# Softmax times values by groups of four query tiles, and a fixed order of VectorE and ScalarE in the last two products

## The chip, the cores and the metric

The kernel runs on one core of a Trainium2 chip. Its engines work side by side and wait for each other by semaphores: TensorE (PE; its weight loads are listed apart as PEld), VectorE (DVE), ScalarE (ACT), GpSimd (POOL) and SyncE (SP), which here issues nearly all DMA transfers. The metric is the device time of one execution in microseconds, from a median of several executions. Less is better.

## What is computed

One layer of a hybrid encoder over 1024 positions of width 1024, in float32. What the change touches is the chunked attention (8 heads of 64, chunks of 64 positions, each query sees its own chunk and 8 before) and the last norm:

```python
def chunked_rel_attention(q, k, v, rel_bias):
    ...
    scores = jnp.einsum('bnqhd,bnkhd->bnhqk', qc, kb).astype(jnp.float32) * (dh ** -0.5)
    scores = scores + bias[None, None]
    scores = jnp.where(valid[None, :, None, None, :], scores, jnp.float32(-1e30))
    p = jax.nn.softmax(scores, axis=-1).astype(v.dtype)
    out = jnp.einsum('bnhqk,bnkhd->bnqhd', p, vb)
    ...
        mixed = rms_norm(mixed.reshape(b, s, N_GROUPS, GROUP_DIM), g).reshape(b, s, MIX_WIDTH)
        x = x + jnp.einsum('bse,ed->bsd', mixed, w_out[l])
        hdn = jnp.einsum('bsd,df->bsf', rms_norm(x, mlp_norm_g[l]), w_up[l])
        hdn = jnp.square(jax.nn.relu(hdn))
        x = x + jnp.einsum('bsf,fd->bsd', hdn, w_down[l])
    return rms_norm(x, final_norm_g)
```

## The kernel before, in words

Precision is kept by splitting a float32 operand into a high and a low part (`split`, L51 to L53: ScalarE copies the high part, VectorE subtracts) and multiplying in two or three passes (`mm3`, L63 to L66). The 1024 positions are 8 tiles of 128.

**The attention stage** lies between 140 and 395 us. Eight heads are four pairs `p` with `j` = 0, 1; a step `i` is one query tile `t` of one head, 64 steps in all. For a step, `scores(i)` makes the products of queries and keys in PSUM, `softmax(i)` adds the bias, takes the row's maximum (VectorE, tile `st`) and the exponentials (ScalarE, L485, tile `pr`). `turn(i)` transposes `pr` in blocks of 128 x 128 on TensorE (L506, tile `pt`), and copies them as a high part `pth` (ScalarE, L510) and a low part `ptl` (VectorE, L511). A query tile sees at most five key tiles, so there are one to five blocks per step. `values(m)` multiplies them with the values: `v` holds a value tile's high and low part side by side as weights, and the moving operand is `pth` and then `ptl`. Before, it takes two query tiles at a time: `pth` and `ptl` have two buffers of 1280 columns, ordered by the distance of key and query tile, and for each key tile there are two products, of 256 columns (384 for the first of a block). The upper and lower halves of the result `av` are added (`ol` on ScalarE, L539; `ya` on VectorE, L540). For a block of two query tiles there are 4, 8, 12 or 12 products, depending on how many key tiles lie before it.

The tiles `pt`, `av` and two tiles of the group norm (`ms`, `R`; L417, L431) share the PSUM tag "PT", which has two buffers that are handed out in turn. The next tile but one waits until the readers of the first are done.

Between the steps stands a filler: projections of the next pairs and of the convolution (tiles `k`, `q`, `cg`, `xh`, `bg`, products of 512 columns), of which `fill_to` calls so many that they last through the 64 steps. Their weights are loaded by `Proj.load` and split into `wh` and `wl`. For the pairs' keys and queries the raw weights go into the buffers that `kc` and `qc` of the pair before last leave free (`expand`, L398 to L403). A scheduler then orders each engine's queue by its own estimate of durations, so the order of the code is not the order on the engine; within a queue an engine works strictly in order. A stretch of code can be exempted (`manual_schedule`): there the named engines keep the code's order.

**The last stage** (from about 800 us) multiplies the hidden layer with `w_down` in blocks; `PLAN` lists seven products per block of hidden columns, each for four tiles of 128 rows, twelve products of 512 columns per row tile in the last block. In the last two products of the last block, the sum of a row tile is complete after `add` (L876). `finish` (L1172 to L1185) then takes the squares (ScalarE, L1166), the scaled sum (VectorE, L1176), the power -1/2 (GpSimd, L1178, tile `rf`), writes the two halves of the output tile `o` (VectorE, L1184) and sends them.

Of the kernel before, what the change touches and what calls it, by code (L numbers as in the profile page):

```python
# [8 lines left out]
F32 = mybir.dt.float32  # L9
# [21 lines left out]
def trunk(ctx, tc, x, mix_g, w_in, rb_rev, conv_w, sg_ln_g, sg_ln_b, sg_w, sg_b,  # L31
# [104 lines left out]
    def acc_tile(name, tag=None):  # L136
        if tag is None:
            ring["i"] += 1
            tag = ring["tags"][ring["i"] % len(ring["tags"])]
        return psA.tile([P, 1024 if tag == "S" else HALF], F32, tag=tag, bufs=2,  # L140
                        name=name)[:, :HALF]
# [346 lines left out]

    def turn(i):
        p, j, t, kb0, nfar = where(i)  # L490
        if t % 2 == 0:
            pts[i // 2] = [AP_.tile([P, 1280], F32R, tag=a, bufs=2, name=f"{a}{i}") for a in ("pth", "ptl")]
            for d in ((1, 3), (3,), (), ())[t // 2]:
                for a in pts[i // 2]:
                    G.memset(a.bitcast(F32)[:, d * 256:d * 256 + P], 0.0)
        pth, ptl = pts[i // 2]
        tq = t % 2
        nb = t - kb0 + 1
        pr = prs.pop(i)
        for d0, d1 in ((0, min(nb, 4)), (4, nb)):  # L500
            if d1 <= d0:
                continue
            pt = psA.tile([P, HALF], F32, tag="PT", bufs=2, name=f"pt{i}{d0}")
            for d in range(d0, d1):
                b = nb - 1 - d
                PE.transpose(pt[:, (d - d0) * P:(d - d0 + 1) * P], pr[:, b * P:(b + 1) * P], ident)  # L506
            src = pt[:, 0:(d1 - d0) * P].rearrange("p (d m) -> p d m", m=P)
            dh = pth.rearrange("p (d m) -> p d m", m=256)[:, d0:d1, tq * P:(tq + 1) * P]
            dl = ptl.rearrange("p (d m) -> p d m", m=256)[:, d0:d1, tq * P:(tq + 1) * P]
            A.activation(dh, src, AF.Copy)  # L510
            V.tensor_tensor(dl, src, dh.bitcast(F32), op=ALU.subtract)  # L511

    def values(m):
        p, j, tb = m // 8, m // 4 % 2, m % 4 * 2
        pth, ptl = pts.pop(m)
        av = acc_tile(f"av{m}", "PT")
        kbs = [tb] + [kb for kb in range(max(0, tb - 4), tb)] + [tb + 1]
        for i, kb in enumerate(kbs):
            d0 = max(0, tb - kb)
            q0 = max(0, kb - tb)  # L520
            lhs = v2[p, kb // 4][:, kb % 4, j, :]


            for ph, pt in ((0, pth), (1, ptl)):
                first = i == 0 and ph == 0
                if d0 == 4:
                    rhs = pt[:, 1024:1280].rearrange("p (i c) -> p i c", c=P)
                    dst = av.rearrange("p (i c) -> p i c", c=256)[:, :, 0:P]
                elif q0:
                    rhs, dst = pt[:, P:3 * P], av[:, P:3 * P]  # L530
                else:
                    cnt = 3 if first else 2
                    base = 0 if first else min(d0 * 256, 512)
                    rhs = pt[:, base:base + cnt * 384].rearrange("p (i c) -> p i c", c=384)
                    rhs = rhs[:, :, d0 * 256 - base:d0 * 256 - base + P]
                    dst = av[:, 0:cnt * P].rearrange("p (i c) -> p i c", c=P)
                PE.matmul(dst, lhsT=lhs, rhs=rhs, start=first, stop=(i == len(kbs) - 1 and ph == 1))  # L537
        ol = tmp(f"ol{m}", m=256)[0:HD]
        A.activation(ol, av[HD:P, 0:256], AF.Copy)  # L539
        V.tensor_tensor(ya[p][j * HD:(j + 1) * HD, tb * P:(tb + 2) * P], av[0:HD, 0:256], ol, op=ALU.add)  # L540
        if j == 1 and tb % 4 == 2:
            hf = tb // 4
            gnq.append((hf, group_norm(ya[p][:, half(hf)], p, f"a{p}{hf}", lsum[p, hf])))

    def split_mixed(c, hf, y):
# [37 lines left out]
    def sgu(u, between):  # L583
        sgw = raw_tile([P, 4, P], "sgw")
        load(sgw, sg_w.rearrange("g t s -> t g s"))
        ps = acc_tile("sgwT")
        for g in range(4):
            PE.transpose(ps[:, g * P:(g + 1) * P], sgw[:, g, :], ident)
        wsT = tmp("wsT").rearrange("p (g t) -> p g t", g=4)
        A.activation(wsT, ps.rearrange("p (g t) -> p g t", g=4), AF.Copy)  # L590
        G.affine_select(out=wsT, in_=wsT, pattern=[[0, 4], [1, P]], compare_op=ALU.is_ge,
                        fill=0.0, base=0, channel_multiplier=-1)
        wsh, wsl = [AP_.tile([P, 4, P], F32R, tag="P", bufs=3, name=f"wsT{a}") for a in "hl"]
        split(wsT, wsh, wsl)
        lnr = raw_tile([P, 2, 256], "lnr")
        load(lnr[:, 0, :], sg_ln_g.partition_broadcast(P))
        load(lnr[:, 1, :], sg_ln_b.partition_broadcast(P))
        ln = AP_.tile([P, 2, 256], F32, tag="P", bufs=3, name="ln")
        V.tensor_copy(ln, lnr)

        ws = load_moving(C_SU + 256, 256, "ws", lambda j, kk, m: [
            AP_.tile([P, 5, 256], F32R, tag=t_, bufs=2, name=f"ws{t_}{j}")[:, 0:kk] for t_ in ("pth", "ptl")])
        vh = [big("VY", [P, 2, NT, HD], F32R, f"vh{i}") for i in range(2)]
        vl = [big("VY", [P, 2, NT, HD], F32R, f"vl{i}") for i in range(2)]
        for t in range(NT):
            ps = token_proj(t, ws, 256, f"sv{t}")
            gv = tmp(f"gv{t}", m=256)
            A.activation(gv, ps, AF.Gelu)
            bs = sm.tile([P, 6], F32, tag="bs", name="bs")
            V.bn_stats(bs, gv)  # L610
            mv = sm.tile([P, 2], F32, tag="mv", name="mv")
            V.bn_aggr(mv, bs)
            r = rstd_of(mv[:, 1:2], 1, 1.0)
            V.tensor_scalar(gv, gv, mv[:, 0:1], r, op0=ALU.subtract, op1=ALU.mult)
            V.tensor_tensor(gv, gv, ln[:, 0], op=ALU.mult)
            V.tensor_tensor(gv, gv, ln[:, 1], op=ALU.add)
            g4 = gv.rearrange("p (i g e) -> p i g e", i=2, g=2)
            for i in range(2):
                split(g4[:, i], vh[i][:, :, t, :], vl[i][:, :, t, :])
        ws = load_moving(C_SU, 256, "wu", place_w("wu"))  # L620
        u += [big("VY", [P, 4, 256], F32, f"u{i}") for i in range(2)]
        for t in range(NT):
            ps = token_proj(t, ws, 256, f"su{t}")
            A.activation(u[t // 4][:, t % 4, :], ps, AF.Gelu)
        tc.keep_in_program_order(A.preload_act_table_set("exp_and_others"))
        between()
        for g in range(4):
            ps = acc_tile(f"sg{g}")
            i, j = g // 2, g % 2
            mm3(ps, wsh[:, g, :], wsl[:, g, :], vh[i][:, j].rearrange("p a b -> p (a b)"),  # L630
                vl[i][:, j].rearrange("p a b -> p (a b)"), True, True)
            for hf in range(2):
                us = u[hf][:, :, g * HD:(g + 1) * HD]
                pv = ps[:, hf * 256:(hf + 1) * 256].rearrange("p (a b) -> p a b", b=HD)
                V.scalar_tensor_tensor(us, pv, cols[:, 14 + g:15 + g], us, op0=ALU.add, op1=ALU.mult)
# [87 lines left out]
    for i in range(64):  # L723
# [3 lines left out]
        turn(i)  # L727
        a, b = target(i), target(i + 1)
        fill_to((a + b) / 2)
        if i % 2 == 0 and i >= 2:  # L730
            values(i // 2 - 1)
        if i + 2 < 64:
            scores(i + 2)
        fill_to(b)
# [9 lines left out]
            next(norm)  # L744
        if p == 3 and k in (5, 6):
            split_half(0, (k - 5,))
    values(31)
    fill_to(1000)
    gn_all((0,))
    sgu_rows(u, 0)  # L750
# [417 lines left out]
    def early_half(t, k):  # L1168
        square(t, k)
        V.tensor_scalar(sums[t][:, 2:3], sums[t][:, k:k + 1], 1.0 / D, EPS, op0=ALU.mult, op1=ALU.add)  # L1170

    def finish(t, k):  # L1172

        ss = sums.get(t)
        square(t, k)
        V.scalar_tensor_tensor(ss[:, 3:4], ss[:, k:k + 1], 1.0 / D, ss[:, 2:3], op0=ALU.mult, op1=ALU.add)  # L1176
        r = sm.tile([P, 1], F32, tag="rf", name="rf")
        G.tensor_tensor(r, ss[:, 3:4], mhalf[:, 0:1], op=ALU.pow)  # L1178
        o = E_.tile([P, D], F32, tag="o", bufs=2, name=f"o{t}")
        for i in (k, 1 - k):  # L1180
            if t + 1 == NT and i != k:
# [15 lines left out]
        ready[n] = [down_ops(PLAN[s][0], p) for p in BLOCKS[b]]  # L1197

    load_down(BLOCKS[0], (1,))
    banks = {}  # L1200
    for n, (b, s) in enumerate(steps):
        if n + 1 < len(steps):
            prep(n + 1)
# [7 lines left out]
        m, which, start, (i, k) = PLAN[s]  # L1211
        ops = ready.pop(n)
        last = b == len(BLOCKS) - 1
        for u in range(4):
            sl = slice(u * P, (u + 1) * P)
            if start:
# [2 lines left out]
            for j, (ho, wo_) in enumerate(ops):  # L1219
                mm3(ps, ho[:, 0, sl], ho[:, 1, sl], wo_[:, 0], wo_[:, 1], start and j == 0, j == len(ops) - 1,  # L1220
                    skip_group_check=True)
            t = 4 * i + u
            add(acc[t][:, half(k)], ps, acc[t][:, half(k)])
            if last and m in (2, 7):
                early_half(t, k)
            if last and m == 7 and t + 1 == NT:
                V.tensor_tensor(acc[t][:, half(k)], acc[t][:, half(k)], gfin[:, half(k)], op=ALU.mult)
            if last and m in (3, 4):
                finish(t, k)


_INS = ["x", "mix_norm_g", "w_in", "rel_bias", "conv_w", "sg_ln_g", "sg_ln_b", "sg_w", "sg_b",
# [24 lines left out]
```

## Time and profile before

| | |
|---|---|
| median of 3 runs | 1120.9 us (1120.43 to 1121.08) |
| profiled execution | 1118.65 us, span 1116.9 us |
| busy: PE, DVE, ACT, POOL | 98%, 67%, 49%, 7% |
| PE, mean granted clock | 0.992 |
| PE idle behind a named wait, largest | 4.2 us at the start, 3.7 us in two waits of transposes |
| PE's last product starts | 1105.72 us |

The profile is one execution, taken by the hardware. A row of the timeline has the start and the duration in us, the engine, the line, the operation, output <- inputs, and the form; in brackets stands how long the engine was idle before, and what it then waited for. Durations of matmuls are modelled and overlap the next one, so the distance between starts says what a product costs. The span ends some 4 us behind the last vector instruction, with the last output written.

### The profile page before, as it was taken

The numbers are of one execution on the slowest core, as the hardware profiler recorded it, in microseconds if no ns is written. First come the engines' busy times: TensorE is split into PE (matmuls) and PEld (weight loads), VectorE is DVE, ScalarE is ACT, GpSimd is POOL, SyncE is SP. The second block draws the span as 40 slices with busy tenths as digits, with TensorE's granted clock in tenths as the row PEclk, the third lists the DMA queues.
The fourth block names the chain that finished last, engine by engine and source line by source line (L and its number), as shares of the span: only waits on it lengthen the run. The fifth ranks groups of instructions, "written<-read, shape, count | busy, mean of one in ns | idle before, by whom it ended". The sixth has DMA issues, their size and how long they took to land.

```text
span 1116.9 us, 14983 instructions
## 1 busy us (share of the span) xinstructions
PE 1090.4 (98%) x5377; PEld 911.8 (82%) x5377; DVE 746.9 (67%) x1430; ACT 551.5 (49%) x1094; POOL 73.2 (7%) x131
## 2 busy tenths in 40 slices
PE   7999999999999999999999999999999999999996
PEld 6889987887888788887888888888878888888884
DVE  5526477667676761569766656564499978869775
ACT  5434376555664630467555555555544433434442
POOL 1101023101021210000000000000000000000001
PEclk8999999999999999999999999999999999999998
DMA  7523013021120143452543535353698545263303
GB/s 244 184 68 80 1 24 88 18 53 47 43 58 23 39 151 131 151 208 104 177 172 122 189 115 196 113 189 125 250 340 280 196 165 188 86 207 103 96 20 150
DMA packets 83197, 145.16 MB, mean 130 GB/s; under 512 B 6050, under 2 KB 41652, under 8 KB 83124
## 3 DMA queue, kind: packets, MB, share of 16 engines
q1 hardware_dynamic: 82548, 142.38, 37.8%
q10 hardware_dynamic: 576, 1.84, 0.4%
q8 instruction: 42, 0.69, 0.3%
q14 instruction: 31, 0.25, 0.1%
HBM read 98.58 MB, written 41.42 MB: 125 GB/s over the span
## 4 chain that ended last, share of the span: by engine, by line
PE 85%; DVE 7%; DMA 4%; ACT 2%; issue 1%; POOL 0%; SPq 0%; POOLq 0%; DVEq 0%; ACTq 0%
PE uA L66 5%; PE uA L65 5%; PE uA L64 5%; PE dA L66 5%; PE dA L64 5%; PE dA L65 4%; PE dB L64 3%; PE dB L66 3%; PE dB L65 3%; PE av L537 3%; PE uC L64 2%; PE uC L66 2%; PE uC L65 2%; PE o L64 2%; PE o L65 2%; PE o L66 2%
## 5 line engine op out<-in xcount | busy, mean ns | idle before, releaser
L52 ACT ACTIVATE ho<-hr 128x512 fp32r<-128x512 f32 x112 | 69.0, 623 | 140.7 <-PE dA L66 51.2
L64 PE MATMUL dA<-wo,ho 128*128 128x512 f32 x256 | 99.7, 390 | 0.8 <-ACT ho L52 0.8
L66 PE MATMUL dA<-wo,ho 128*128 128x512 f32 x256 | 99.3, 390 | 0.5 <-DVE ho L53 0.5
L65 PE MATMUL dA<-wo,ho 128*128 128x512 f32 x256 | 99.5, 389 | 0.0
L53 DVE TENSOR_TENSOR ho<-hr,ho 128x512 fp32r<-128x512 f32 x112 | 76.8, 690 | 15.7 <-ACT ho L52 15.7
L64 PE MATMUL dB<-wo,ho 128*128 128x512 f32 x192 | 74.8, 390 | 0.0
L66 PE MATMUL dB<-wo,ho 128*128 128x512 f32 x192 | 74.8, 390 | 0.0
L65 PE MATMUL dB<-wo,ho 128*128 128x512 f32 x192 | 74.7, 389 | 0.0
L53 DVE TENSOR_TENSOR wo<-wd,wo 128x512 fp32r<-128x512 f32 x96 | 65.6, 689 | 2.3 <-ACT wo L52 2.3
L52 ACT ACTIVATE wo<-wd 128x512 fp32r<-128x512 f32 x96 | 58.8, 619 | 10.1 <-DVE wd L879 6.2
L485 ACT ACTIVATE pr<-s,st 128x640 f32<-128x640 f32 (+2 forms) x64 | 42.3, 661 | 36.9 <-DVE st L480 26.6
L64 PEld LDWEIGHTS dA<-wo,ho 128*128 128x128 f32 x256 | 48.0, 188 | 11.3 <-ACT ho L52 1.5
L66 PEld LDWEIGHTS dA<-wo,ho 128*128 128x128 f32 x256 | 48.0, 188 | 11.1 <-DVE ho L53 1.1
L65 PEld LDWEIGHTS dA<-wo,ho 128*128 128x128 f32 x256 | 48.1, 188 | 9.9
L510 ACT ACTIVATE pth<-pt 128x512 fp32r<-128x512 f32 (+2 forms) x96 | 40.0, 435 | 32.1 <-PE pt L506 31.4
L876 DVE TENSOR_TENSOR acc<-dA,acc 128x512 f32<-128x512 f32 x64 | 43.8, 690 | 16.7 <-PE dA L66 15.0
L511 DVE TENSOR_TENSOR ptl<-pt,pth 128x512 fp32r<-128x512 f32 (+2 forms) x96 | 45.2, 487 | 12.9 <-ACT pth L510 11.9
L64 PE MATMUL o<-woh,mxh 128*128 128x512 f32 x128 | 50.6, 399 | 0.0
L66 PE MATMUL o<-woh,mxl 128*128 128x512 f32 x128 | 50.0, 391 | 0.0
L65 PE MATMUL o<-wol,mxh 128*128 128x512 f32 x128 | 50.0, 390 | 0.0
L1178 POOL TENSOR_TENSOR rf<-ssf,mhalf 128x1 f32<-128x1 f32 x8 | 4.4, 551 | 617.4 <-DVE ssf L1176 617.4
L876 DVE TENSOR_TENSOR hid<-uC,v 128x512 f32<-128x512 f32 x15 | 10.4, 691 | 51.5 <-PE uC L66 51.5
(344 smaller groups left out, 3083.0 us busy)
## 6 DMA issues: line engine op xcount, KB each, us to landing
wr_u<-in_w_up SPq DMA_DIRECT2D x32, 512.0 KB, 4.3
wd<-in_w_down SPq DMA_DIRECT2D x32, 512.0 KB, 4.6
wr_o<-in_w_out SPq DMA_DIRECT2D x8, 512.0 KB, 4.3
xr<-in_x SPq DMA_DIRECT2D x8, 512.0 KB, 4.9
hs<-h SPq DMA_DIRECT2D x8, 512.0 KB, 3.7
acc<-hs SPq DMA_DIRECT2D x16, 256.0 KB, 6.5
out_y<-o SPq DMA_DIRECT2D x16, 256.0 KB, 2.1
x<-in_x SPq DMA_DIRECT2D x7, 512.0 KB, 3.9
```

Source lines behind the costliest of these rows:

```text
L52: A.activation(hi, raw, AF.Copy)
L53: V.tensor_tensor(lo, raw, hi.bitcast(F32), op=ALU.subtract)
L64: PE.matmul(ps, lhsT=sh, rhs=mh, start=start, stop=False, **kw)
L65: PE.matmul(ps, lhsT=sh, rhs=ml, start=False, stop=False, **kw)
L66: PE.matmul(ps, lhsT=sl, rhs=mh, start=False, stop=stop, **kw)
L485: A.activation(pr[:, :b - a], s[:, a:b], AF.Exp, bias=st[:, 2:3], accum_out=lsum[p, t // 4][:, lc:lc + 1])
L510: A.activation(dh, src, AF.Copy)
L511: V.tensor_tensor(dl, src, dh.bitcast(F32), op=ALU.subtract)
L537: PE.matmul(dst, lhsT=lhs, rhs=rhs, start=first, stop=(i == len(kbs) - 1 and ph == 1))
L876: V.tensor_tensor(out, a, b, op=ALU.add)
L1178: G.tensor_tensor(r, ss[:, 3:4], mhalf[:, 0:1], op=ALU.pow)
```

## The change

`values` takes four query tiles at a time. `pth` and `ptl` become two tags each, one for the first half of a head's query tiles (13 blocks of 128 columns) and one for the second (22), one buffer each. In the second half, the block of distance `d` of query tile `q` stands at column block 1 + 4d + q, with a block of zeros at 0 and at 21, so that the products for the first and the last key tile also have at least 256 columns. In the first half the blocks are ordered by key tile, with one block of zeros (at 11). For each key tile there are again two products, now of 256, 384 or 512 columns; the moving operand reads its blocks at steps of 1, 4 or 5 blocks, and the result is one run of columns. There are 16 blocks of products in place of 32. `ol` and `ya` work on 512 columns. `values(m)` is called every fourth step.

In the last two products VectorE and ScalarE keep the order of the code. `finish` is taken apart: `rate` (scaled sum and power) of a row tile comes ahead of the `add` of the next one, `finish` (the two writes) behind it.

```diff
+        hf, tq = t // 4, t % 4
+        if tq == 0:
+            pts[i // 4] = [AP_.tile([P, (22 if hf else 13) * P], F32R, tag=f"{a}{hf}", bufs=1, name=f"{a}{i}")
+                           for a in ("pth", "ptl")]
+            for a in pts[i // 4]:
+                for z in (0, 21) if hf else (11,):
+                    G.memset(a.bitcast(F32)[:, z * P:(z + 1) * P], 0.0)
...
-                b = nb - 1 - d
+                b = nb - 1 - d if hf else d
...
+            dh, dl = [blocks(a, *((1 + 4 * d0 + tq, 4) if hf else (tq, 3)), d1 - d0) for a in (pth, ptl)]
...
+    def blocks(a, first, step, count):
+        n = a.shape[1] // P
+        a = a.rearrange("p (n m) -> p n m", m=P)
+        return a[:, first:min(n, first + step * (count - 1) + 1):step]
...
-        kbs = [tb] + [kb for kb in range(max(0, tb - 4), tb)] + [tb + 1]
+        kbs = [tb] + [kb for kb in range(max(0, tb - 4), tb + 4) if kb != tb]
         for i, kb in enumerate(kbs):
             lhs = v2[p, kb // 4][:, kb % 4, j, :]
+            q0, q1 = max(tb, kb), min(tb + 4, kb + 5)
             for ph, pt in ((0, pth), (1, ptl)):
+                if kb == tb + 3:
+                    rhs, dst = blocks(pt, *((0, 4) if hf else (11, 1)), 2), av[:, 2 * P:4 * P]
+                elif kb == tb - 4:
+                    rhs, dst = blocks(pt, 17, 4, 2), av[:, 0:2 * P]
                 else:
+                    rhs = blocks(pt, *((1 + 4 * (q0 - kb) + q0 - tb, 5) if hf else (3 * kb + q0, 1)), q1 - q0)
+                    dst = av[:, (q0 - tb) * P:(q1 - tb) * P]
...
-            AP_.tile([P, 5, 256], F32R, tag=t_, bufs=2, name=f"ws{t_}{j}")[:, 0:kk] for t_ in ("pth", "ptl")])
+            AP_.tile([P, 4, 256], F32R, tag=f"{t_}{j}", bufs=1, name=f"ws{t_}{j}")[:, 0:kk] for t_ in ("pth", "ptl")])
...
-        if i % 2 == 0 and i >= 2:
-            values(i // 2 - 1)
+        if i % 4 == 0 and i >= 4:
+            values(i // 4 - 1)
...
+        if n + 2 == len(steps):
+            man.enter_context(tc.manual_schedule(engines={mybir.EngineType.Activation, mybir.EngineType.DVE}))
...
+            if whole:
+                rate(*whole[0])
             add(acc[t][:, half(k)], ps, acc[t][:, half(k)])
...
             if last and m in (3, 4):
-                finish(t, k)
+                square(t, k)
+                whole.append((t, k))
+                if len(whole) > 1:
+                    finish(*whole.pop(0))
+    rate(*whole[0])
+    finish(*whole.pop())
+    man.close()
```

What this does to the engines' queues at two places follows. The first is ScalarE where the heads of pair 1 begin, before the change. `pr` are exponentials (of the next pair's first query tiles from `pr_2040` on), `pth` copies of transposed blocks (the last query tile of pair 0 is copied from `pt_2042` and `pt_2049`), `wh_k` the split of the key weights of pair 2, loaded into `kc`:

```order
L510 ACTIVATE pth_1990<-pt_2042 128x4x128
L52 ACTIVATE wh_k_1967<-kc_1717 128x1024
L510 ACTIVATE pth_1990<-pt_2049 128x128
L485 ACTIVATE pr_2083,lsum_2029<-s_2059,st_2080 128x256
L510 ACTIVATE pth_2085<-pt_2091 128x128
```

The same place with the change:

```order
L512 ACTIVATE pth_1834<-pt_1990 128x4x128
L512 ACTIVATE pth_1834<-pt_1997 128x128
L485 ACTIVATE pr_1988,lsum_1977<-s_1978,st_1985 128x128
L52 ACTIVATE wh_k_1933<-kc_1689 128x1024
L485 ACTIVATE pr_2031,lsum_1977<-s_2007,st_2028 128x256
L512 ACTIVATE pth_2033<-pt_2037 128x128
```

The second copy of the last query tile moved from behind the weights' split to ahead of it. The other place is VectorE in the last two products, for two row tiles in the middle, before the change (`acc` sums, `ssf` the scaled sum of squares, `o` the output):

```order
L876 TENSOR_TENSOR acc_7553<-dB_9798,acc_7553 128x512
L1176 SCALAR_TENSOR_TENSOR ssf_9624<-ssf_9624 128x1
L1184 SCALAR_TENSOR_TENSOR o_10018<-acc_7553,rf,gfin 128x512 x2
L876 TENSOR_TENSOR acc_7555<-dB_9812,acc_7555 128x512
L1176 SCALAR_TENSOR_TENSOR ssf_9642<-ssf_9642 128x1
L1184 SCALAR_TENSOR_TENSOR o_10041<-acc_7555,rf,gfin 128x512 x2
```

And with it:

```order
L878 TENSOR_TENSOR acc_7361<-dB_9606,acc_7361 128x512
L1188 SCALAR_TENSOR_TENSOR o_9820<-acc_7359,rf,gfin 128x512 x2
L1177 SCALAR_TENSOR_TENSOR ssf_9432<-ssf_9432 128x1
L878 TENSOR_TENSOR acc_7363<-dB_9620,acc_7363 128x512
L1188 SCALAR_TENSOR_TENSOR o_9843<-acc_7361,rf,gfin 128x512 x2
```

The writes of a row tile moved behind the add of the next one.

## Rows read from the trace of the kernel before

**Rows 1.** The page, busy us, share of the span, instructions of an engine:

```profile
PE 1090.4 (98%) x5377; PEld 911.8 (82%) x5377; DVE 746.9 (67%) x1430; ACT 551.5 (49%) x1094; POOL 73.2 (7%) x131
```

**Rows 2.** Who waited for whom, TensorE, whole span: total us, times, longest:

```profile
PE xT L218 <- DVE xn L231: 4.2, 1, 4.2
PE pt L506 <- DVE ptl L511: 3.7, 2, 1.9
PE uA L66 <- DVE a1l L53: 1.4, 1, 1.4
```

**Rows 3.** The view of tile av: duration ns (min/median/max), first and last start, forms:

```profile
L537 PE MATMUL av<-pth,v x144: 278/283/522, 145.9 to 392.6; 128*128 128x256 f32 x112, 128*128 128x384 f32 x32
...
L537 PE MATMUL av<-ptl,v x144: 274/283/415, 146.2 to 392.7; 128*128 128x256 f32 x144
L539 ACT ACTIVATE ol<-av x32: 382/382/385, 146.8 to 393.1; 64x256 f32<-64x256 f32 x32
L540 DVE TENSOR_TENSOR ya<-av,ol x32: 406/417/419, 147.2 to 393.9; 64x256 f32<-64x256 f32 x32
```

**Rows 4.** Timeline of TensorE at a block of four products and the scores behind it:

```profile
145.93 0.42 PE L537 MATMUL av<-pth,v 128*128 128x384 f32 x1
146.19 0.27 PE L537 MATMUL av<-ptl,v 128*128 128x256 f32 x1
...
146.54 0.34 PE L463 MATMUL s<-kh,q 128*128 128x384 f32 x1
146.71 0.34 PE L464 MATMUL s<-kl,q 128*128 128x384 f32 x1
```

**Rows 5.** Timeline of TensorE, last products of two row tiles:

```profile
1081.24 0.39 PE L66 MATMUL dA<-wo,ho 128*128 128x512 f32 x1
...
1105.72 0.39 PE L66 MATMUL dA<-wo,ho 128*128 128x512 f32 x1
```

**Rows 6.** Timeline of VectorE in the tail:

```profile
1081.66 0.69 DVE L876 TENSOR_TENSOR acc<-dA,acc 128x512 f32<-128x512 f32 x1 [1.02 <-PE dA L66]
...
1105.68 0.16 DVE L1176 SCALAR_TENSOR_TENSOR ssf<-ssf 128x1 f32<-128x1 f32 x1 [0.85 <-ACT sq L1166]
1106.50 1.42 DVE L1184 SCALAR_TENSOR_TENSOR o<-acc,rf,gfin 128x512 f32<-128x512 f32 x2 [0.67 <-POOL rf L1178]
...
1109.44 0.69 DVE L876 TENSOR_TENSOR acc<-dA,acc 128x512 f32<-128x512 f32 x1
```

**Rows 7.** The chain of waits, 186 to 200 us (start, us, what):

```profile
186.29 5.91 DMA kc<-in_w_in
...
192.22 1.07 ACT wh_k L52
...
193.32 1.22 DVE wl_k L53
194.54 0.21 DVE ptl L511
...
194.80 0.33 PE pt L506
```

**Rows 8.** Timelines of VectorE, ScalarE and TensorE at both heads' changes:

```profile
194.66 0.74 DVE L432 SCALAR_TENSOR_TENSOR ya<-Ra,cols,ya 128x512 f32<-128x512 f32 x1
...
198.40 0.64 ACT L409 ACTIVATE sqa<-ya 128x512 f32<-128x512 f32 x1
...
199.87 0.95 PE L417 MATMUL msa<-onesel,sqa 128*128 128x2 f32 x8
...
258.37 0.33 PE L506 MATMUL pt<-ident,pr 128*128 128x128 f32 x1 [1.80 <-DVE ptl L511]
...
262.65 1.05 PE L417 MATMUL msa<-onesel,sqa 128*128 128x2 f32 x8
```

**Rows 9.** The chain of waits at the end of the attention stage:

```profile
382.40 0.88 DVE ptl L511 x2
...
390.80 2.17 PE av L537 x12
```

**Rows 10.** Stretches there: us, busy us of engines, granted PE clock, DMA:

```profile
384.80:388.80 4.00, 2.01 (x18) 1.61 (x16) 3.92 (x8) 3.89 (x8) 0.00 (x0) 1.00 0.37 131
388.80:392.20 3.40, 3.40 (x14) 3.11 (x15) 2.31 (x4) 1.81 (x3) 2.55 (x1) 0.50 0.10 26
```

More of the change, by code (lines that the diff above doesn't have):

```diff
@@ L490, in turn @@
         p, j, t, kb0, nfar = where(i)
[L491 to L497, printed above, removed]
+        hf, tq = t // 4, t % 4
[5 more added lines that the diff above has]
+                    G.memset(a.bitcast(F32)[:, z * P:(z + 1) * P], 0.0)
+        pth, ptl = pts[i // 4]
         nb = t - kb0 + 1
@@ L504, in turn @@
             for d in range(d0, d1):
-                b = nb - 1 - d
+                b = nb - 1 - d if hf else d
                 PE.transpose(pt[:, (d - d0) * P:(d - d0 + 1) * P], pr[:, b * P:(b + 1) * P], ident)
             src = pt[:, 0:(d1 - d0) * P].rearrange("p (d m) -> p d m", m=P)
-            dh = pth.rearrange("p (d m) -> p d m", m=256)[:, d0:d1, tq * P:(tq + 1) * P]
-            dl = ptl.rearrange("p (d m) -> p d m", m=256)[:, d0:d1, tq * P:(tq + 1) * P]
+            dh, dl = [blocks(a, *((1 + 4 * d0 + tq, 4) if hf else (tq, 3)), d1 - d0) for a in (pth, ptl)]
@@ L510, in turn @@
             A.activation(dh, src, AF.Copy)
             V.tensor_tensor(dl, src, dh.bitcast(F32), op=ALU.subtract)
+    def blocks(a, first, step, count):
+        n = a.shape[1] // P
+        a = a.rearrange("p (n m) -> p n m", m=P)
+        return a[:, first:min(n, first + step * (count - 1) + 1):step]
     def values(m):
-        p, j, tb = m // 8, m // 4 % 2, m % 4 * 2
+        p, j, hf = m // 4, m // 2 % 2, m % 2
         pth, ptl = pts.pop(m)
+        tb = 4 * hf
         av = acc_tile(f"av{m}", "PT")
-        kbs = [tb] + [kb for kb in range(max(0, tb - 4), tb)] + [tb + 1]
+        kbs = [tb] + [kb for kb in range(max(0, tb - 4), tb + 4) if kb != tb]
@@ L518, in values @@
         for i, kb in enumerate(kbs):
-            d0 = max(0, tb - kb)
-            q0 = max(0, kb - tb)
             lhs = v2[p, kb // 4][:, kb % 4, j, :]
+            q0, q1 = max(tb, kb), min(tb + 4, kb + 5)
             for ph, pt in ((0, pth), (1, ptl)):
[L525 to L530, printed above, removed]
-                else:
[L532 to L542, printed above, removed]
+                if kb == tb + 3:
+                    rhs, dst = blocks(pt, *((0, 4) if hf else (11, 1)), 2), av[:, 2 * P:4 * P]
+                elif kb == tb - 4:
+                    rhs, dst = blocks(pt, 17, 4, 2), av[:, 0:2 * P]
+                else:
+                    rhs = blocks(pt, *((1 + 4 * (q0 - kb) + q0 - tb, 5) if hf else (3 * kb + q0, 1)), q1 - q0)
+                    dst = av[:, (q0 - tb) * P:(q1 - tb) * P]
@@ L543, in values @@
+                PE.matmul(dst.rearrange("p (i c) -> p i c", c=P), lhsT=lhs, rhs=rhs, start=i == 0 and ph == 0,
+                          stop=(i == len(kbs) - 1 and ph == 1))
+        ol = tmp(f"ol{m}")[0:HD]
+        A.activation(ol, av[HD:P], AF.Copy)
+        V.tensor_tensor(ya[p][j * HD:(j + 1) * HD, half(hf)], av[0:HD], ol, op=ALU.add)
+        if j == 1:
             gnq.append((hf, group_norm(ya[p][:, half(hf)], p, f"a{p}{hf}", lsum[p, hf])))
@@ L746, in trunk @@
             split_half(0, (k - 5,))
-    values(31)
+    values(15)
     fill_to(1000)
@@ L1170, in early_half, with rate @@
         V.tensor_scalar(sums[t][:, 2:3], sums[t][:, k:k + 1], 1.0 / D, EPS, op0=ALU.mult, op1=ALU.add)
-    def finish(t, k):
[L1174 to L1178, printed above, removed]
+    def rate(t, k):
+        ss = sums[t]
+        V.scalar_tensor_tensor(ss[:, 3:4], ss[:, k:k + 1], 1.0 / D, ss[:, 2:3], op0=ALU.mult, op1=ALU.add)
+        rates[t] = sm.tile([P, 1], F32, tag="rf", name="rf")
+        G.tensor_tensor(rates[t], ss[:, 3:4], mhalf[:, 0:1], op=ALU.pow)
+    def finish(t, k):
+        r = rates[t]
         o = E_.tile([P, D], F32, tag="o", bufs=2, name=f"o{t}")
@@ L1199, in trunk @@
     load_down(BLOCKS[0], (1,))
-    banks = {}
+    banks, whole, rates, man = {}, [], {}, ExitStack()
     for n, (b, s) in enumerate(steps):
```

## The prediction

> **What bounds the kernel now.** I read the page's busy shares first: TensorE is busy for 98% of the span [rows 1]. Since a matmul's end is modelled, that alone proves little, so next came the view of who waited for whom, TensorE alone. Its largest wait in the attention stage (140 to 395 us) is two waits of transposes, 3.7 together; its largest behind that stage is 1.4 [rows 2]. So a matmul saved in the attention stage is time saved, unless a wait opens in its place, and all that follows moves forward with it. The timeline's tail tells the second thing: TensorE's last product starts at 1105.72 [rows 5], yet the span ends at 1116.9. There VectorE decides [rows 6].
>
> **Durations.** They come from one profiled execution of 1118.65 us (span 1116.9); the median of the runs shown is 1120.9, 2.25 more. I take the saving from the trace and subtract it from the median.
>
> **Part A, products of softmax rows and values.** The view by tile counts 32 products of 384 columns and 112 + 144 of 256 [rows 3]: per head four blocks of 4, 8, 12 and 12. The change makes two blocks per head. From its loops: 8 products for the first half (2 of 512 columns, 2 of 384, 4 of 256) and 16 for the second (4, 4, 8). Times eight heads that is 48 of 512, 48 of 384 and 96 of 256: 192 products instead of 288, and 67,584 columns instead of 77,824. The price of one is the distance between starts, not the listed duration: 0.117 for 256 columns (146.19 to 146.54, three products), 0.17 for 384 [rows 4], 0.227 for 512 (108 products from 1081.24 to 1105.72) [rows 5]. Before: 32 x 0.17 + 256 x 0.117 = 35.4. After: 48 x 0.227 + 48 x 0.17 + 96 x 0.117 = 30.3. That is 5.1 us. A block's first product takes longer than its width: 0.26 to the next start where 0.17 would be due [rows 4]. At 0.07 for each of 16 blocks fewer, 1.1 more. **A = 6.2**, bounds 5.1 and 7. The moving operand now has gaps of several blocks; the old one had gaps too, and its products keep the 0.117, so I price them at nothing.
>
> **Edits at nothing.** The zero blocks: 6 clears per head as before, 48 in all, on GpSimd, issued four query tiles ahead of their use. Uncovered, a clear would only stand in front of a block's last products. Copy and add out of PSUM: 16 pairs of double width instead of 32, on engines with slack. The spatial gating's weights move to the two new tags, two tiles as before. Behind the first output products TensorE's order is as it was.
>
> **Part B, the tail.** Before, VectorE adds tile t, waits 0.85 for ScalarE's squares, then 0.67 for GpSimd's power, and only then writes both halves [rows 6]. So it falls behind TensorE, and the last add starts at 1109.44. In the new order the rate of tile t-1 stands ahead of the add of t, and its two writes behind it. Per tile VectorE then has 0.16 + 0.69 + 1.42 = 2.27 us of work [rows 6] with nothing to wait for but TensorE, which needs 12 x 0.227 = 2.72. An add that waits for TensorE starts 0.42 after the last product's start (1081.24 to 1081.66) [rows 5, 6]: the last then at 1105.72 + 0.42 = 1106.14. What follows (squares, power, two halves, output) has the same links as before, 1116.9 - 1109.44 = 7.46. **B = 1109.44 - 1106.14 = 3.3**. If VectorE could not keep the pace, 0 would be left; I see no work that would stop it.
>
> **Part C, the two waits of transposes.** The chain of waits shows the first as one thing [rows 7]: the next pair's key weights load into a buffer that VectorE's kl has just left (5.91), ScalarE and VectorE split them (1.07, 1.22), and behind these stands the ptl that frees a PSUM buffer for a transpose. In the new order both copies of a head's last tile stand ahead of the split, and TensorE has the block of 16 products to do before it needs what stands behind it. The load is no faster, so I follow the chain on to the group norm's small products, msa. From wl_k's end (194.54) to the squares that msa needs (198.40) took 3.86 [rows 7, 8]; of it the ya of 0.74 now stands ahead of wl_k, and the block's copy and add are 0.5 longer (part E). With the squares' 0.64 that is 4.26: msa at 198.8, before at 199.87 [rows 8]. Of the 1.07 gained, 0.5 are columns of A. The second place: 258.1 + 4.26 = 262.4 against 262.65 [rows 8], but with two products of the k projection more done ahead of it (0.45), so 0.7, of which 0.5 again belong to A. **C = 0.6 + 0.2 = 0.8**; ends: 3.7 if both waits go for good, -1 if what now stands behind the split is missed sooner.
>
> **Part D, the end of attention.** The 12 products that stood between the last two tiles' transposes now come behind them, in the block of 16. VectorE's work sets its start: after ptl (382.40 + 0.88 = 383.28 [rows 9]) the new order has a weight split (1.22, as wl_k [rows 7]), a mxl (about 0.7), the last tile's ptl (0.9), a mxl and a ya (0.7 each): 387.5. At full clock the block would be through at 390.1; the old one of 12 ran from 390.80 for 2.17 [rows 9]. But the granted clock was 1.2 GHz from 388.8 to 392.2 and 2.4 until then [rows 10]. If that stretch comes where it came, 1.7 us of products are lost in it, and the stage ends where it ended, columns apart. **D = 0**, ends -2.6 (rival 2) and +1.4. The Trainium skill speaks against the change here: "TensorE: Matmul & The Clock Gate", Part 4, says that transposes don't count as TensorE's work for the clock in the way that products do. By that rule the longer stretch of transposes alone lets the clock fall sooner; the trace neither shows nor excludes it, since there the clock stayed full for 4 us after a block of products had ended. The sum by it is rival 2's.
>
> **Part E, the double-width block in PSUM.** It holds one of the two buffers that the transposes need until copy and add are done. They took 0.38 and 0.42 for 256 columns [rows 3]; an add of 512 took 0.69 [rows 6], and for the copy I estimate 0.6 by the same step. So each hold is 0.5 longer. The new order has about as many fillers behind a block as before, so I take 0.02 for each of 16. **E = -0.3**, ends 0 and -4 (half of the blocks, 0.5 each).
>
> **Sum.** 6.2 + 3.3 + 0.8 + 0 - 0.3 = 10.0: the profiled run would be 1108.65, the median 1120.9 - 10.0 = **1110.9**.
>
> **Rivals.** (1) The waits at the heads' changes vanish: C = 3.7, 1108.0. For: TensorE now has 2.6 us of products there. Against: the load's chain, above. (2) The clock is low through the whole last block, 2.56 us of products by part A's prices, which half the clock doubles: 1113.5. For: no dense product between 382 and 387 in the new order. Against: the 4 us at full clock [rows 10]. The page's rule named in part D is this case. (3) The held PSUM buffer: the place is the transposes behind each of the 16 blocks, the mechanism a TensorE wait for the add that frees the buffer. At 0.25 each it costs 4 us: 1114.6. From 0.65 each it eats the whole gain, from 0.8 the kernel is measurably slower; at 1.0 it is 16 us: 1126.6. For: the fillers were placed for shorter holds. Against: TensorE's largest waits of before name ptl, not this add [rows 2]. (4) The fixed order doesn't do what it says and VectorE waits in the tail as before: B = 0, 1114.2. Against: the order in the section on the change.
>
> **How the numbers follow.** The forecast (1109.5 to 1112.5) gets 0.58, rival 1 0.12, rival 2 0.10, rival 3 at its small price 0.10 and at its large one 0.04, rival 4 0.04, no change 0.02. The range of 8 in 10 reaches from rival 1 with A at its upper bound (1107.2), and a little below for D, to rival 3's small price and a little above: **1106.5 to 1115.5**. 0.2% (2.2 us) is about what a measurement of this kernel can tell from no change. All but the large price and no change end below 1118.7: faster 0.94, same 0.02, slower 0.04.
>
> **What the changed profile would show.** A: 192 products with values, in forms of 512, 384 and 256, at 0.227, 0.17 and 0.117 from start to start; if the gaps cost, these distances grow. B: adds 0.42 behind TensorE's last product, no wait of VectorE for squares or power until the last tile; the span ends 11 us behind TensorE's last start. C: no wait of a transpose near 2 us beside the key weights' load; instead up to 1 us ahead of msa. D: granted clock between 380 and 392. E: waits of transposes for ya. The forecast is wrong if the stage from 140 to 395 shortens by less than 4 us, or if TensorE waits for ya add up to more than 2 us.

## The result and the profile after

The changed kernel takes 1107.91 us (median of 4 runs, 1105.73 to 1108.85), where the kernel before took 1120.66 beside it (median of 4): a ratio of 0.989, 95% interval 0.9874 to 0.9906. That is 1.1% faster, at 1110.9 forecast, within the range of 1106.5 to 1115.5. Its profiled execution took 1108.38 (span 1106.6), against 1118.65 (span 1116.9) of before: 10.3 less, 10.0 forecast. The medians lie 12.75 apart since the profiled run of before was 2.0 below its own median, and that of after 0.5 above its own. On two further chips the ratio was 0.9912 (0.9894 to 0.993) and 0.9893 (0.9874 to 0.9912), medians 9.8 and 11.6 apart. Each interval reaches some 2 us to either side, more than the 0.3 between 10.3 and 10.0.

The page of after, busy us and share of the span, against [rows 1]:

```profile
PE 1084.8 (98%) x5281; PEld 904.9 (82%) x5281; DVE 745.3 (67%) x1414; ACT 546.2 (49%) x1078; POOL 72.7 (7%) x131
```

TensorE's busy time fell by 5.6 only, the span by 10.3; the rest are waits and the tail (and the busy time of after holds more products at the low clock, see part D). Who waited for whom, TensorE (total us, times, longest), against [rows 2]:

```profile
PE xT L218 <- DVE xn L231: 4.1, 1, 4.1
PE dA L64 <- ACT ho L52: 2.0, 1, 2.0
PE Ra L431 <- DVE ptl L513: 1.9, 1, 1.9
...
PE msa L417 <- ACT sqa L409: 0.8, 1, 0.8
PE s L466 <- DVE s L465: 0.6, 1, 0.6
```

The two waits of transposes for ptl (3.7) are gone, and no wait for ya has come. New are 0.8 ahead of a group norm's small products (msa), at the first head change, and 0.6 ahead of scores (s), at 172. The wait ahead of Ra, at the end of attention, grew from 1.1 to 1.9. Before, a transpose there also waited for ya, which the prediction passed over:

```profile
PE Ra L431 <- DVE ptl L511: 1.1, 1, 1.1
PE pt L506 <- DVE ya L540: 0.9, 1, 0.9
```

The tile view of av (duration ns, first and last start, forms), against [rows 3]:

```profile
L539 PE MATMUL av<-pth,v x96: 274/337/774, 152.4 to 384.3; 128*128 128x256 f32 x48, 128*128 128x512 f32 x24, 128*128 128x384 f32 x24
...
L542 ACT ACTIVATE ol<-av x16: 593/595/597, 154.5 to 385.0; 64x512 f32<-64x512 f32 x16
L543 DVE TENSOR_TENSOR ya<-av,ol x16: 677/683/685, 155.2 to 385.6; 64x512 f32<-64x512 f32 x16
```

192 products, in the forms of part A. To see where the 10.3 came from, I set the same instruction of both traces side by side (start in us):

| place | before | after | ahead by |
|---|---|---|---|
| one of the last sg products, ahead of attention | 135.89 | 136.49 | -0.6 |
| msa, first norm of attention | 182.54 | 183.03 | -0.5 |
| msa at the first head change | 199.87 | 198.97 | 0.9 |
| msa between the changes | 245.20 | 243.07 | 2.1 |
| msa at the second head change | 262.65 | 258.57 | 4.1 |
| msa near the end of attention | 378.75 | 371.11 | 7.6 |
| first transposes of the MLP | 449.33 | 442.44 | 6.9 |
| TensorE's last product | 1105.72 | 1098.87 | 6.85 |
| end of the span | 1116.9 | 1106.6 | 10.3 |

Attention up to the msa near its end gave 8.2, the rest up to the MLP took back 0.75, the long middle of the kernel moved along unchanged, and the tail gave 3.45. The 0.6 at the start was lost ahead of anything that the change touches; in the other profiles with the new attention (but for the one with four copies) the msa of the first norm starts between 182.0 and 184.6, so it lies within that scatter.

### The profile page after: what moved, and what is told of

Read it like the earlier page. It is cut to its first block, busy times and chain, and to the rows that moved or that the text cites. A ratio compares the mean times of both kernels' runs of the same rounds, so it can differ in the third digit from the quotient of the medians.

```text
span 1106.6 us, 14740 instructions
## 1 busy us (share of the span) xinstructions
PE 1084.8 (98%) x5281; PEld 904.9 (82%) x5281; DVE 745.3 (67%) x1414; ACT 546.2 (49%) x1078; POOL 72.7 (7%) x131
## 4 chain that ended last, share of the span: by engine, by line
PE 89%; DVE 4%; DMA 4%; ACT 2%; issue 1%; SPq 0%; POOLq 0%; POOL 0%; DVEq 0%; ACTq 0%
PE dA L64 5%; PE dA L66 5%; PE dA L65 5%; PE uA L66 4%; PE uA L65 4%; PE uA L64 4%; PE dB L64 4%; PE dB L66 4%; PE dB L65 4%; PE o L64 3%; PE av L539 3%; PE o L66 3%; PE o L65 3%; PE uC L64 2%; PE uC L65 2%; PE uC L66 2%
## 5 line engine op out<-in xcount | busy, mean ns | idle before, releaser
L52 ACT ACTIVATE wo<-wd 128x512 fp32r<-128x512 f32 x96 | 58.7, 618 | 11.2 <-DVE wd L881 7.5
L485 ACT ACTIVATE pr<-s,st 128x640 f32<-128x640 f32 (+2 forms) x64 | 42.3, 660 | 31.6 <-DVE st L480 27.2
L513 DVE TENSOR_TENSOR ptl<-pt,pth 128x512 fp32r<-128x512 f32 (+2 forms) x96 | 44.9, 485 | 10.9 <-ACT pth L512 10.5
```

What stands on the lines that cost most here:

```text
L52: A.activation(hi, raw, AF.Copy)
L485: A.activation(pr[:, :b - a], s[:, a:b], AF.Exp, bias=st[:, 2:3], accum_out=lsum[p, t // 4][:, lc:lc + 1])
```

## Experiments

Every kernel was timed beside the kernel before on its own chip; ratios are to that.

**1. The two parts apart.** First the kernel before with the tail of the changed kernel:

```
-                finish(t, k)
+                square(t, k)
+                whole.append((t, k))
+                if len(whole) > 1:
+                    finish(*whole.pop(0))
...
```

(Cut: `rate` of the tile before ahead of the `add`, and the fixed order, as in the change.)

> The kernel before with the new order of the last two products alone; attention as before. Part B's theory: TensorE's last product is where it was, each add starts about 0.42 us behind TensorE's last product of its tile, and the span ends about 7.9 us behind TensorE's last start instead of 11.2: 3.3 to 3.5 us less than before. Rival: the order costs something elsewhere (a split or an add that now stands behind a write), and less than 2 us are gained.

Then the changed kernel with the old tail:

> The changed kernel with the old order of the last two products; the groups of four alone. Theory: 7 us less than before (the changed kernel's profile puts TensorE's last start 6.9 earlier), and 3.3 to 3.5 more than the changed kernel; the two parts add up. Rival: TensorE's earlier end and the tail's order depend on each other (the medians of before and after lie 12.8 apart, their profiles only 10.3), so that this part alone gives more than 9 or less than 5.

The tail alone: 1115.45 against 1120.14, ratio 0.9964 (0.9948 to 0.998). The values alone: 1112.38, ratio 0.9938 (0.9914 to 0.9962). In microseconds 4.0 and 6.9 by the ratios; together 10.9, within what the whole change gives. So within these intervals (some 2 us each) the parts add, and neither needs the other. VectorE's last adds with the tail alone:

```profile
1102.14 0.69 DVE L876 TENSOR_TENSOR acc<-dA,acc 128x512 f32<-128x512 f32 x1 [0.64 <-PE dA L66]
1104.86 0.69 DVE L876 TENSOR_TENSOR acc<-dA,acc 128x512 f32<-128x512 f32 x1 [0.64 <-PE dA L66]
```

They come 2.72 apart and wait for TensorE, whose last product started at 1104.44 here: 0.42 ahead. The span ended at 1112.2, 7.8 behind that product; with the values alone it was 11.2 (1100.80 to 1112.0), as before. That is 3.4 for the tail, in both kernels.

**2. The code of the tail without the fixed order.**

```
-            man.enter_context(tc.manual_schedule(engines={mybir.EngineType.Activation, mybir.EngineType.DVE}))
+            pass
```

> The changed kernel with the new code of the last two products but without the fixed order: the scheduler then puts most writes of tile t-1 ahead of the add of tile t on VectorE. Theory: VectorE waits again for squares and power ahead of these writes, so the add comes late: a tile takes about 0.69 + 0.85 + 0.16 + 0.67 + 1.42 = 3.8 us where both writes stand ahead, 3.1 where one does, against TensorE's 2.72, and nearly all of the 3.3 is lost again: 3 to 4 us more than the changed kernel. Rival: writing the code in the new order is enough, the same time as the changed kernel within 1 us.

1113.92, ratio 0.9946 (0.9931 to 0.9962), where the changed kernel has 0.989 to 0.9912. VectorE in its tail:

```profile
1100.58 0.16 DVE L1177 SCALAR_TENSOR_TENSOR ssf<-ssf 128x1 f32<-128x1 f32 x1 [0.85 <-ACT sq L1168]
...
1104.42 1.41 DVE L1188 SCALAR_TENSOR_TENSOR o<-acc,rf,gfin 128x512 f32<-128x512 f32 x2 [0.66 <-POOL rf L1179]
1105.76 0.68 DVE L878 TENSOR_TENSOR acc<-dA,acc 128x512 f32<-128x512 f32 x1
```

Both writes of the tile before stand ahead of the last add (of every other tile one does), the waits for squares and power [rows 6] are back, and the last add starts at 1105.76, 5.3 behind TensorE's last product; the span ends 12.3 behind it (1100.43 to 1112.7) instead of 7.7. The gain is in the order itself; code written in that order but left to the scheduler loses it: the span ends 1.1 later behind TensorE than in the kernel before.

**3. Gaps in the moving operand.**

```
+                rhs = blocks(pt, hf, 1, dst.shape[1] // P)
```

> The changed kernel with the moving operand of each product of softmax rows and values read from neighbouring blocks of columns instead of blocks that lie 3, 4 or 5 apart: as many columns, but the wrong ones, so that attention's result is not computed. Theory (part A): the gaps cost nothing, the products start 0.227, 0.17 and 0.117 apart as with gaps, the same time within 0.5 us. Rival: the gaps cost, the distances shrink by 5% or more, and the time by 1.5 us or more.

1108.36, ratio 0.9913 (0.9889 to 0.9937); the changed kernel beside it 1109.32. TensorE inside a block of 16:

```profile
255.98 0.39 PE L540 MATMUL av<-ptl,v 128*128 128x512 f32 x1
256.21 0.34 PE L540 MATMUL av<-pth,v 128*128 128x384 f32 x1
...
256.57 0.28 PE L540 MATMUL av<-pth,v 128*128 128x256 f32 x1
256.69 0.28 PE L540 MATMUL av<-ptl,v 128*128 128x256 f32 x1
```

From one start to the next 0.23 for 512 columns, 0.18 (0.36 for two) for 384 and 0.12 for 256. The changed kernel's own block, with gaps:

```profile
255.14 0.40 PE L539 MATMUL av<-ptl,v 128*128 128x512 f32 x1
255.38 0.34 PE L539 MATMUL av<-pth,v 128*128 128x384 f32 x1
...
255.73 0.28 PE L539 MATMUL av<-pth,v 128*128 128x256 f32 x1
255.85 0.28 PE L539 MATMUL av<-ptl,v 128*128 128x256 f32 x1
```

The same distances within 0.01. Steps of four and five blocks cost nothing that these two runs can tell.

**4. Key weights loaded early, in the kernel before.**

```
-    SLOTS = {"N": 16, "QK": 6, "QC": 2, "VY": 10}
+    SLOTS = {"N": 16, "QK": 6, "QC": 3, "VY": 10}
```

> The kernel before with a third buffer for the raw key and query weights, so that no pair's key weights wait for the subtraction kl to leave a buffer; the products are those of before. Theory of part C: the late load is what stands behind the two waits of transposes (1.9 and 1.8), both go, and TensorE is 3 to 3.7 us ahead behind the second head change; of that up to 1 us may be lost at the start, where the second pair's key weights now load among the rows of x. Rival: the waits come from the number of split and copy steps in VectorE's order there, another step stands in the same place, and less than 1.5 us are gained.

1115.73 against 1120.25, ratio 0.9953 (0.9936 to 0.9971). From 180 to 275 us TensorE had the two waits for ptl in the kernel before [rows 2]; its waits there with the third buffer:

```profile
PE av L537 <- DVE ptl L511: 0.4, 2, 0.2
PE pt L506 <- DVE ya L540: 0.2, 1, 0.2
```

Both waits are gone. By the places of the table TensorE gains 1.4 at the first change (msa at 199.01 where it was at 199.87, after a start 0.6 later) and 1.8 at the second: 3.2 of the 3.7. So the late load is the cause of these two waits, and the changed kernel gains on the same waits that this one removes. Both at once were not run.

**5. A longer hold of the PSUM buffers.** The copy out of PSUM twice, then four times:

```
-        A.activation(ol, av[HD:P], AF.Copy)
+        for _ in range(2):
+            A.activation(ol, av[HD:P], AF.Copy)
```

> The changed kernel with the copy out of each block's PSUM buffer made twice: every one of 16 buffers is held 0.5 to 0.6 us longer. Theory (part E): there is slack behind the blocks, TensorE waits for none of the 16 adds, and the time is that of the changed kernel within 1 us. Rival 3: the hold stands on TensorE's path, and the time grows by 0.3 to 0.6 for each block, 5 to 9 us.

> The changed kernel with the copy out of each block's PUSM buffer made four times: each of the 16 buffers is held about 1.7 us longer. Theory: the slack behind a block is about one further transpose group (1.7 to 3.2 us to the second next transposes in the changed kernel's timeline, against a hold of 1.6 to 2.5 as it stands), so this goes beyond it: TensorE waits for about half of the 16 adds, 3 to 8 us more than the changed kernel. Rival: the slack reaches further and the time stays within 1 us.

Twice: 1109.65, ratio 0.9915 (0.9895 to 0.9936), the changed kernel beside it 1109.32. Four times: 1115.36, ratio 0.9953 (0.9935 to 0.9971), the changed kernel beside it 1108.69. So 0.6 more per buffer costs nothing that the medians tell, 1.8 more costs some 6.7. With two copies TensorE waits for no ya, but the trace is not the changed kernel's otherwise: a wait of 1.3 stands behind the key weights' split at 254, and at the end of attention the clock stayed at 2.4 GHz, which gives 1.9 back (part D). So a cost of 1 us could hide in these medians. TensorE's waits with four copies:

```profile
PE pt L509 <- DVE ptl L513: 1.3, 2, 0.8
PE msa L417 <- ACT sqa L409: 1.3, 3, 0.6
...
PE pt L509 <- DVE ya L544: 0.7, 3, 0.3
```

Only 0.7 is the buffer that I had in mind; the expected waits for half of the 16 adds did not come. The three rows add up to 3.3 of the 6.7. The 48 added copies are some 29 us of ScalarE's time, the scheduler placed other work differently around them, and this profile also has a low-clock stretch of 3.4 us at 825. How much the hold alone would cost at that length stays open.

**6. The end of attention.** Twelve products that nobody reads keep TensorE occupied there, on two chips:

```
...
+    dum = wide("dum")
+    for i in range(12):
+        PE.matmul(dum[:, 0:HALF], lhsT=v2[3, 0][:, 0, 0, :], rhs=dzs[0][:, 0:HALF], start=True, stop=True)
     values(15)
```

> The changed kernel with 12 products of 512 columns that nobody reads added at the end of attention, 7 ahead of the last tile's transposes and 5 behind them, where TensorE waited 1.9 us and did only transposes and small products for 5 us. Theory (rival 2 of the prediction came true): the granted clock stays at 2.4 GHz, the last block of 16 takes 2.6 us instead of 4.8, and of these 2.2 us some is given back by the 7 products that stand in the way (up to 1.6): 0.5 to 2 us less than the changed kernel. Rival: the block is slow for another reason (its operands come late), the block stays at 4.8, and the time is the same or up to 2.7 us more.

> The changed kernel with the 12 products that nobody reads at the end of attention, as dense12, now beside the changed kernel on one chip. Theory: the clock of the last block costs 1.2 to 1.3 us on the path and no more, since the output products behind it wait for their split weights: 1.2 less than the changed kernel. Rival: the whole 2.2 of the block, or nothing.

> The changed kernel itself once more, beside the three other runs on this chip: 10 to 11 us less than before.

First the stretches of the changed kernel (us, TensorE's busy us, granted clock, DMA), from its last dense products on:

```profile
373.16:378.95 5.79, 3.55 (x28) 1.00 0.18 53
379.01:385.81 6.80, 6.80 (x26) 0.50 0.28 102
```

The same place with the twelve products:

```profile
379.50:382.16 2.66, 2.66 (x19) 1.00 0.04 15
382.16:386.00 3.84, 2.82 (x14) 1.00 0.11 15
```

The clock stays at 2.4 GHz, and the last block takes 2.66 instead of 4.84. But TensorE is idle for 1.0 of the next 3.84. Its waits there:

```profile
PE o L65 <- DVE wol L53: 0.6, 1, 0.6
PE o L64 <- ACT woh L52: 0.4, 1, 0.4
```

The output products stand and wait for the split output weights, so in the trace only 1.3 is won behind it (the next group norm's msa starts at 395.33 instead of 396.61). These waits are in part the experiment's own doing: the scheduler put the twelve products ahead of the transposes uT, and ScalarE, which splits the weights behind their copies (mxh), had to wait for them; in the changed kernel these copies start at 375.92 and 377.12.

```profile
379.35 1.27 ACT L666 ACTIVATE mxh<-uT,cols 128x512 fp32r<-128x512 f32 x2 [2.32 <-PE uT L664]
```

In the medians nothing is to be seen: 1109.34 (ratio 0.9903, 0.9881 to 0.9924) on one chip; 1109.21 on the other, beside 1108.69 of the changed kernel, where 1.2 less was expected. The changed kernel itself was 11.6 ahead of the kernel before on that chip, a little more than expected.

The other way to fill the place, with useful products held back from earlier:

```
-            ((0, 0), (2, 6), (12, 38), (16, 48)) if p < 3 else ((0, 0), (2, 6), (15, 55))
+            ((0, 0), (2, 6), (12, 38), (16, 48)) if p < 3 else ((0, 0), (2, 6), (15, 50))
```

> The changed kernel with one number of the plan changed: the last head's knot (15, 55) is (15, 50), so that four or five steps of the convolution gate's projection (12 to 15 products of 512 columns, 2.7 to 3.4 us) stand behind the last tile's transposes instead of being done before. Theory: useful products fill TensorE's wait of 1.9 us and hold the granted clock at 2.4 GHz through the last block (2.6 us instead of 4.8): 1.2 us less than the changed kernel, as the added products gave, and up to 3 more where the wait is really filled. Rival: the output products stand and wait for the split output weights and the mixed rows in any case, the gate's group norm comes later too, and nothing is gained or up to 2 us are lost.

> The changed kernel itself, on the chip of the three runs that it is compared with here. Theory: 10 to 12.5 us less than before, as its profile (10.3) and its medians (12.8) have it.

1112.97, ratio 0.9941 (0.9922 to 0.996), beside 1109.32 of the changed kernel (ratio 0.9912, 0.9894 to 0.993; 9.8 less than before, a little under what was expected): 3.7 slower by the medians. The rival's mechanism was right, and the loss larger than its 2 us. ScalarE there, and TensorE's one wait:

```profile
379.25 1.26 ACT L663 ACTIVATE mxh<-uT,cols 128x512 fp32r<-128x512 f32 x2
...
381.96 2.00 ACT L52 ACTIVATE woh<-wr_o 128x1024 fp32r<-128x1024 f32 x2
```

```profile
PE o L64 <- ACT woh L52: 4.1, 1, 4.1
```

The last block was done at 378.1, 6.6 earlier than in the changed kernel, and the output products began at 384.01, 0.7 earlier. ScalarE works without a pause up to that point. So in this order, where the gate's products and with them uT come late, ScalarE's list of splits sets the end of attention, not TensorE; and in the wait of 4.1 the clock fell all the same. That is not the whole loss: at the first transposes of the MLP this trace is only 1.2 behind the changed kernel's on the same chip (444.15 against 442.93). The rest comes later, with a low-clock stretch of 3.4 us at 810 among it.

## Why the forecast held, step by step

**Part A: right.** Forecast 6.2. The 8 blocks of eight products took 1.30 to 1.41, seven blocks of sixteen 2.57 to 2.59; the old ones 0.52 to 0.61 (four), 1.00 to 1.12 (eight) and 1.48 to 1.60 (twelve). With the last block of each kernel, where the clock was low, counted at 2.58 and 1.5, that is 31.6 instead of 37.5: 5.9. Of it 5.4 lie ahead of the msa near the end of attention and 0.5 behind. The price of nothing for the gaps is borne out by experiment 3.

**Part B: right.** Forecast 3.3, measured 3.45 in the changed kernel and 3.4 alone. VectorE in the tail of after, against [rows 6]:

```profile
1098.51 0.15 DVE L1177 SCALAR_TENSOR_TENSOR ssf<-ssf 128x1 f32<-128x1 f32 x1
1099.29 0.69 DVE L878 TENSOR_TENSOR acc<-dA,acc 128x512 f32<-128x512 f32 x1 [0.64 <-PE dA L66]
1099.90 1.40 DVE L1188 SCALAR_TENSOR_TENSOR o<-acc,rf,gfin 128x512 f32<-128x512 f32 x2
...
1102.04 0.75 DVE L1188 SCALAR_TENSOR_TENSOR o<-acc,rf,gfin 128x512 f32<-128x512 f32 x1 [0.66 <-POOL rf L1179]
```

The add waits for TensorE alone, as the six ahead of it do, 0.42 behind its product; the one wait for the power is the last tile's. My sentence that the span would end 11 us behind TensorE's last start was a slip: that is the kernel before. The part's own terms give 0.42 + 7.46 = 7.9, and 7.7 was measured.

**Part C: waits right, size wrong.** Forecast 0.8, measured 2.8 (the 8.2 of attention up to the msa near its end, less part A's 5.4 there). Most of it can be read directly: between the same two marks TensorE was idle for 4.4 before and for 2.0 after. The first head change went as forecast: msa at 198.97, forecast 198.8, behind a wait of 0.8 for the squares where up to 1 was announced (the split itself ended 0.4 later than the forecast had it, and what follows took 0.25 less):

```profile
197.57 0.69 DVE ya L543
...
198.29 0.64 ACT sqa L409
...
198.97 1.05 PE msa L417 x8
```

The step that failed is the second place, 262.4 forecast and 258.57 measured. I left the end of wl_k at 258.1, where the kernel before had it. But the chain to it starts with kl, which stands behind work that had moved forward with the gains made until then. The split's two ends, before and then after, VectorE:

```profile
248.82 1.22 DVE L400 TENSOR_TENSOR kl<-kc,kh 64x1024 fp32r<-64x1024 f32 x1
...
256.89 1.23 DVE L53 TENSOR_TENSOR wl_k<-kc,wh_k 128x1024 fp32r<-128x1024 f32 x1 [2.17 <-ACT wh_k L52]
```

```profile
246.68 1.22 DVE L400 TENSOR_TENSOR kl<-kc,kh 64x1024 fp32r<-64x1024 f32 x1
...
253.81 1.22 DVE L53 TENSOR_TENSOR wl_k<-kc,wh_k 128x1024 fp32r<-128x1024 f32 x1 [0.50 <-ACT wh_k L52]
```

kl came 2.1 earlier, the load took 0.9 less (4.8 instead of 5.7), wl_k came 3.1 earlier, and the wait of 1.80 [rows 8] went whole. The load's length is not the change's doing: the kernel with the old attention and the new tail had 4.7 there, and its two waits came to 2.1 instead of 3.7:

```profile
PE pt L506 <- DVE ptl L511: 2.1, 2, 1.4
```

So the waits' price differs from one execution to the next. Rival 1 was nearer for the second place, my own chain for the first.

**Part D: event of rival 2, at half its price.** Forecast 0 columns apart, measured -1.25: the -0.75 of the table holds 0.5 of part A's columns. Rival 2's event came: the clock was at 1.2 GHz from 379.0 on, through the whole last block of 16:

```profile
378.17 0.63 PE Ra L431 x4
378.80 1.21 PE msb L417 x8
380.01 4.90 PE av L539 x16
```

What failed is the premise that the low stretch comes where it came: it was 6.8 us long instead of 3.4. What goes with that length can be read from the other profiles (us at 1.2 GHz at the end of attention; us from the msa near the end to the first transposes of the MLP):

| kernel | low clock | to the MLP |
|---|---|---|
| before; old attention with the new tail | 3.4 | 70.58; 70.53 |
| old attention with a third buffer | 6.8 | 72.17 |
| changed, three profiles; values alone | 6.8 | 71.32 to 71.33; 71.34 |
| experiments 2 and 3 | 3.4 | 70.02; 70.07 |
| two copies out of PSUM | none | 69.39 |
| twelve added products, two chips | none | 70.04; 70.17 |

With 3.4, as before, the new attention takes 0.5 less, which is the columns: then D is 0, as forecast. The longer stretch costs 1.3, where rival 2 had 2.6. With none, in the kernel with two copies, 1.9 are won (its splits also stand in another order). There the output products follow the block at once:

```profile
380.00 0.47 PE L539 MATMUL av<-pth,v 128*128 128x512 f32 x1
...
382.66 0.40 PE L64 MATMUL o<-woh,mxh 128*128 128x512 f32 x1
```

The block is through in 2.7 instead of 4.84, but a wait of 1.0 comes up behind it, of transposes for VectorE's yb:

```profile
PE uT L662 <- DVE yb L432: 1.0, 1, 1.0
```

I had nowhere asked in this part what is late next. The Trainium skill's rule that I cited ("TensorE: Matmul & The Clock Gate", Part 4: transposes don't count as TensorE's work as products do) is not settled by these runs. On its side, the clock fell behind 5.8 us of nearly only transposes, small products and idle time (2.2 of them idle), and stayed up in both profiles with twelve products among them; without these it fell at the end of attention in eight of nine profiles of the new attention. Against it, in the kernel with two copies it stayed up behind the same transposes, and the old attention also had 6.8 us once. So that the change itself brought the longer stretch is not shown.

**Part E: nothing instead of -0.3.** Copy and add took 0.595 and 0.683 as estimated; TensorE waits for no ya, and for none with 0.6 more either (experiment 5). Rival 3 is out at this hold, though its mechanism exists: the kernel before had a wait of 0.9 for ya, which my reading of [rows 2] left out.

**The sum.** 5.9 + 3.45 + 2.8 - 1.25 - 0.6 (start) = 10.3, forecast 10.0. Errors of opposite sign, C by +2.0 against D by -1.25 and the start's 0.6, nearly cancelled: that the total came out within 0.3 is luck. That A and B came out is not. Rival 4 is out for the change as made; experiment 2 is that rival, and it costs 4.5 in the profile, where the forecast had 3.3.

## What to carry to other kernels

A chain that starts behind work that gets faster starts earlier itself: take the whole chain forward, not only its end. Before pricing a slow stretch, look for what would end next without it, and read its price from traces that differ in that stretch: here 1.3 instead of 2.6. Work added to fill a wait can itself hold back what the next stage waits for: see first what it will stand in front of. Where a program's scheduler decides the order, writing the code in a better order may change nothing: look at the order, then fix it.

## What the runs showed of the hardware

The low clock doesn't come alike in every execution of the same work. At the end of attention three profiles of the changed kernel had 1.2 GHz for 6.8 us, as had the values alone; the kernels of experiments 2 and 3, with the same order of products, for 3.4; two copies out of PSUM for none. Counted from where the dense products end, it fell after 5.8 us in the changed kernel (373.16 to 379.0) and after 7.6 us in experiment 3 (374.42 to 382.0), with the same transposes and waits between. Such a stretch also comes up elsewhere, in single executions: with the twelve products on the second chip it came at 515, behind a wait of 2.3 us,

```profile
515.71 0.79 PE L66 MATMUL uA<-mh,a1l 128*128 128x512 f32 x1 [2.26 <-DVE a1l L53]
```

and with the code order left to the scheduler at 514. In the first of these TensorE was at half its clock:

```profile
515.60:519.00 3.40, 3.29 (x8) 0.50 0.54 157
```

Such stretches may be behind some of the 2 us between two executions of one kernel, as between the profiles and medians here; this was not shown.
